# Two products' operands stay in SBUF, the other loads come three to a product from one list, and the splits of SwiGLU's results and the second norm's sums come later

## The chip, the cores and the metric

One core of a Trainium2 chip runs the kernel. The metric is the device time of one execution in microseconds (us); less is better.

## The reference

One layer of a hybrid decoder on x of 512 tokens by 2048 channels in float32. The input projection and the mixers come first and are not touched by the change. The change lies in the last line, the feed-forward part, with D_FF = 5632:

```python
h = rms_norm(x, norm1_g)
aq, ak, av, bu, bg, cq, ck, cv = split(h @ w_in)
mix = concat(dilated attention A, conformer convolution B, sliding attention C)
x = x + mix @ w_out
h2 = rms_norm(x, norm2_g)                       # "norm2": one factor per token
x = x + (silu(h2 @ w_gate) * (h2 @ w_up)) @ w_down
```

## The kernel before, in words

**Number form.** Each float32 operand of TensorE is split into a high part (fp32r) and the rest: for weights wh and wl (tiles of 128x1024), for activations two halves of one tile h or a. ScalarE (ACT) casts a weight tile twice, once into PSUM (wn, L275) and once into SBUF (wh, L276); VectorE (DVE) subtracts to get wl (L277). `split_up_to` does this two units ahead of use.

**Products.** The feed-forward matrix products are cut by a scheme of seven products for a 2x2 block product: instead of eight block products there are seven, on sums of blocks. They come in the order 5, 1, 7, 6, 2, 4, 3 (`ORDER`); below, "product 0" to "product 6" is the place in this order and "q" the number. The sums of weights, w('s'), w('21') and so on, are made by GpSimd (POOL, L211) from raw blocks w('11'), w('12'), w('21'), w('22') that SyncE (SP) loads at L259. The last number in such a name is the unit, of which a product has two. The sums of activations were made earlier and written to DRAM (hd, seven per pair of chunks).

**Steps.** 22 steps w0 to w21 (class `Wide`) make gate and up, eight steps d0 to d7 (class `Turned`) the first 16 pairs of chunks of the down product, and eight more (class `Down`) the rest. Each step w or d is seven products of 24 matmuls of 128x512 at L1383. Two steps, an odd w and the even one after it, use the same half of h: four of the eight pairs of chunks, so 4 x 7 = 28 tiles of 256 KB are in SBUF. In each even step w2 to w20, when a product has used its four tiles for the last time, these are freed, and one product later the four of the other half are loaded for the same q (`load_ops`, `h<-hd`, L1584). In w21 the same happens with four loads of a per product for d0 (`load_act`, `a<-od`, L1578).

**The results of two steps.** In an odd step g the blocks of gate and up get complete; `finish` (L1519 to L1521) makes silu(gate) x up for one of four blocks, turns it and sends it to DRAM (zd). At the end of the odd step each of the two chunks of features (named f with its number: f14 and f15 for w15) is set up to be read back, as `r` at one product's delay and as `l` at four (L1299, 64-element pieces), summed by POOL (`sums1`: ta, `sums2`: tb, L1307 to L1314), split by ACT and DVE (`piece`, L1319 to L1327) and stored to DRAM (od), from which the steps d load a. `piece3` splits r, `piece4` the needed half of l, `piece1` ta, `piece2` tb. The numbers in `PIECES_AT` are the delays in products of sums1, sums2, piece3, piece4, piece1, piece2, for the two chunks.

**What sets the order.** Everything is written out by hand in one program order, and each engine works through its own instructions in that order. `later(n, fn)` puts work into a queue that is run n products on, after the product's matmuls. SP issues all the transfers one after another. At each product `next_unit` also lets SP load the next raw blocks of weights as their buffers come free (`pump`). `slot` takes one of N_SLOTS tiles of 128x512; a tile is free again when its last reader is done.

**Norm2.** In w0, after product 2, `norm2` lets DVE copy the sums of squares (ssum2b, L1230) and TensorE add them over partitions (n2s, L355).

Of the kernel before, what the change touches and what calls it, by code (L numbers as in the profile page):

```python
# [16 lines left out]
T = 512  # L17
# [30 lines left out]
        "bg2 cq2 cq7 ak2 cq4 cq6 bu3 bg3 ak0 aq0 ak1 aq1 aq2 ak3 aq3").split()  # L48
ROWS = "c0 c3 c1 c5 c2 c7 c4 c6 a0 a1 b2 b1 b0 b3 a2 a3".split()

N_SLOTS = 67
N_WIDE = 4
COLUMN_BANKS = 2

# [23 lines left out]
J_SET = NJ // 2  # L78


PIECES_AT = ((5, 6, 2, 6, 6, 7), (6, 7, 4, 7, 8, 11))


BY = 4
# [42 lines left out]
def kernel(ctx: ExitStack, tc: tile.TileContext, xT, wi, wo, wgu, wd, cst_in, outT):  # L127
# [21 lines left out]
    def slot(name, dt=F32, cols=T):  # L149
        return sp.tile([P, cols], dt, name=name, tag="s")  # L150
# [78 lines left out]
    def set_of(g):  # L229
        return (g + 1) // 2 % 2  # L230
# [851 lines left out]
    def halves(t):  # L1082
        return t[:, :TH], t[:, TH:]
# [139 lines left out]

    outs = [(bank if i < 4 - COLUMN_BANKS else column)(f"out{i}") for i in range(4)]

    def norm2():
        b = psum["high"].tile([P, 1024], F32, name="n2s", tag="h")
        by_rows = slot("ssum2b")
        for v, to in zip(halves(ssum2), halves(by_rows)):
            nc.vector.tensor_copy(by_block(to), v.rearrange("p (a b c) -> p a b c", b=2, c=32))  # L1230
        n2["r"] = token_scale(by_rows, D, "n2", b[:, :NT])[1]

    acts = {}
    od = {p: tc.dram_tile([P, 7 * T], F32, name=f"od{p}") for p in range(NP)}
# [218 lines left out]
    class Wide(Turned):  # L1453
# [55 lines left out]
        def finish(self, at):  # L1509
            y, half = self.y.pop(at), int(at[1]) - 1  # L1510
            s, z = slot(f"s{self.g}_{at}"), slot(f"z{self.g}_{at}")
            gate = psum["high"].tile([P, 1024], F32, name=f"s{self.g}n{at}", tag="h")
            to = z.rearrange("p (b h c) -> p b h c", b=8, h=2)
            for h, t in enumerate(y):
                both = t.rearrange("p (f m d) -> p f m d", f=2, m=2)
                cols = slice(h * TH, (h + 1) * TH)
                act, out = (v[:, cols].rearrange("p (f d) -> p f d", f=2) for v in (gate, s))
                scale = n2["r"][:, 2 * half + h:2 * half + h + 1]
                nc.scalar.activation(act, both[:, :, 0], AF.Silu, scale=scale)  # L1519
                nc.vector.scalar_tensor_tensor(out, both[:, :, 1], scale, act, op0=ALU.mult, op1=ALU.mult)  # L1520
                nc.vector.transpose(to[:, :, h], s[:, cols].rearrange("p (c b) -> p b c", b=8))  # L1521
            later(0, nc.sync.dma_start, self.zd[at[0] == at[1]][{"12": 0, "21": 1, "22": 0, "11": 1}[at]], z,
                  queue=extras)
# [53 lines left out]
            at = LAID.index(q)  # L1577
            nc.sync.dma_start(acts[q, j].bitcast(F32), od[j][:, at * T:(at + 1) * T])  # L1578

    def load_ops(q, which):  # L1580
        for j in range(J_SET * which, J_SET * (which + 1)):
            ops[q, j] = slot(f"h{q}_{j}", F32R)
            at = LAID.index(q)
            nc.sync.dma_start(ops[q, j].bitcast(F32), hd[j][:, at * T:(at + 1) * T])  # L1584

    blk = None
    rest = [(q, j) for q in ORDER for j in range(TURNED, NP)]
    for g in range(G_STEPS + N_DOWN):
        t = g - G_STEPS
        turned = 0 <= t < N_TURNED  # L1590
        if t < 0:
            blk = Wide(g, blk)
        else:
            blk = (Turned if turned else Down)(t)
        for i, q in enumerate(ORDER):
            sums_now()
            run(evacs)
            for sub in range(BY // 2 if t < N_TURNED else 1):
                w = next_unit()
                if t < 0:  # L1600
                    first = J_SET * set_of(g) + 2 * sub
                    blk.multiply(i, sub, w, [ops[q, j] for j in range(first, first + 2)])
                    if ticks.due:
                        ticks.tick()
                elif turned:
                    first = BY * (t // 2) + 2 * sub
                    blk.multiply(i, sub, w, [acts[q, j] for j in range(first, first + 2)])
                else:
                    blk.multiply(q, w, [acts[q, j] for j in range(TURNED, NP)])
            if g == 0 and i == 2:  # L1610
                norm2()

            if t < 0 and (g % 2 == 0 or t == -1):
                for j in range(J_SET * set_of(g), J_SET * (set_of(g) + 1)):
                    ops.pop((q, j))
                if g == 0 and i == 0:
                    held.pop("x1"), held.pop("x3")
                    opening_ops.clear()
                if t == -1:
                    later(1, load_act, q, range(BY), queue=extras)  # L1620
                elif g:
                    later(1, load_ops, q, 1 - set_of(g), queue=extras)
            elif turned and t % 2:
                first = BY * (t // 2)
                for j in range(first, first + BY):
                    acts.pop((q, j))
                first += BY
                if first < TURNED:
                    later(1, load_act, q, range(first, first + BY), queue=extras)
            if N_TURNED - 2 <= t < N_TURNED:  # L1630
                n = 4 - (t % 2 == 0)
                for q2, j in rest[:n]:
                    later(1 if t % 2 else 0, load_act, q2, [j], queue=extras)
                del rest[:n]
            if i == (5 if turned else 3):
                load_y(t + 1)
            run(extras)
# [85 lines left out]
```

## Time and profile before

| what | value |
|---|---|
| median of 3 runs | 1888.57 us (1888.47 to 1890.7) |
| the profiled execution | 1890.46 us |
| its span, first to last instruction | 1888.7 us |
| mean granted clock of TensorE | 0.997 |
| read from HBM / written | 329.87 MB / 80.22 MB |
| loads h<-hd | 280 of 256 KB |

The profile is of one execution. TensorE's row (PE) in the stretches below is its matmuls alone; "[2.35 <-DVE ssum2b L1230]" behind an instruction says that its engine was idle for 2.35 us before it, and that a result of DVE's line 1230 ended that. PEclk is the share of full clock that TensorE was granted. SPq rows are the issue of a transfer, not its course.

### The profile page before, as it was taken

What the parts mean: (1) busy time and instruction counts of PE and PEld (TensorE: products, weight loads), DVE (VectorE), ACT (ScalarE), POOL (GpSimd) and SP (SyncE); (2) the same over time, 40 slices, a digit from 0 to 9 for tenths busy, and PEclk for the clock granted to TensorE, in tenths of its full rate; (3) what the DMA queues carried; (4) which work ended last, traced back from release to release, by engine and by line L of the source; (5) the groups of instructions that cost most, each with busy time, mean ns of one, the idle gap of its engine ahead of it and who ended that gap; (6) DMA issues with size and microseconds to landing.
All of it is one profiled execution on the core that took longest, in us unless ns stands there. A gap on an engine that the chain in (4) does not pass through costs nothing.

```text
span 1888.7 us, 26860 instructions
## 1 busy us (share of the span) xinstructions
PE 1861.3 (99%) x8548; PEld 1539.6 (82%) x8548; DVE 1530.9 (81%) x2318; ACT 1360.4 (72%) x1956; POOL 1083.9 (57%) x681
## 2 busy tenths in 40 slices
PE   9999999999999999999999999999999899999999
PEld 7888888888887887788887888878887788888888
DVE  7688899897578788788887888978878677778887
ACT  6234555555456788888888888888877887777775
POOL 6013445362253458576585765856757676776786
PEclk9999999999999999999999999999999999999999
DMA  6334333433396377989879898798979595678984
GB/s 258 134 106 117 96 95 101 117 123 117 115 321 238 108 231 258 291 263 312 261 253 300 262 309 266 245 310 263 310 243 349 179 335 184 206 244 284 310 242 124
DMA packets 330077, 419.49 MB, mean 222 GB/s; under 512 B 82256, under 2 KB 211408, under 8 KB 329936
## 3 DMA queue, kind: packets, MB, share of 16 engines
q1 hardware_dynamic: 329792, 417.77, 68.6%
q8 instruction: 68, 1.11, 0.2%
q14 instruction: 73, 0.60, 0.1%
q10 hardware_dynamic: 144, 0.01, 0.0%
HBM read 329.87 MB, written 80.22 MB: 217 GB/s over the span
## 4 chain that ended last, share of the span: by engine, by line
PE 78%; DMA 5%; DVE 5%; ACT 4%; POOL 3%; issue 2%; SPq 2%; DVEq 0%; POOLq 0%; ACTq 0%
PE out L1383 44%; PE out L1275 6%; PE o L313 2%; PE o L315 2%; PE o L314 2%; DMA h<-hd 2%; PE cq L313 2%; PE cq L314 2%; PE cq L315 2%; SPq L1584 1%; DVE G L1483 1%; ACT wn L275 1%; DMA a<-od 1%; DVE wl L277 1%; ACT wh L276 1%
## 5 line engine op out<-in xcount | busy, mean ns | idle before, releaser
L1383 PE MATMUL out<-wh,h 128*128 128x512 f32 x2464 | 616.1, 392 | 11.2 <-ACT wh L276 10.1
L1383 PEld LDWEIGHTS out<-wh,h 128*128 128x128 f32 x2464 | 462.0, 188 | 118.2 <-ACT wh L276 19.2
L1383 PE MATMUL out<-wl,h 128*128 128x512 f32 x1232 | 330.2, 390 | 0.0
L1383 PEld LDWEIGHTS out<-wl,h 128*128 128x128 f32 x1232 | 231.8, 188 | 48.4
L1383 PE MATMUL out<-wh,a 128*128 128x512 f32 x896 | 223.3, 391 | 7.3 <-ACT wh L276 7.2
L1383 PEld LDWEIGHTS out<-wh,a 128*128 128x128 f32 x896 | 168.2, 188 | 45.3 <-ACT wh L276 10.2
L1383 PE MATMUL out<-wl,a 128*128 128x512 f32 x448 | 120.6, 391 | 0.0
L1383 PEld LDWEIGHTS out<-wl,a 128*128 128x128 f32 x448 | 84.7, 189 | 17.7
L515 DVE SCALAR_TENSOR_TENSOR y<-bu,cst,y 128x511 f32<-128x511 f32 (+14 forms) x120 | 93.8, 781 | 1.4
L1486 DVE TENSOR_TENSOR G<-G,out 128x512 f32<-128x512 f32 x132 | 83.6, 674 | 3.9 <-PE out L1383 3.9
L271 ACT CAST wh<-w 128x1024 fp32r<-128x1024 f32 (+1 forms) x41 | 42.1, 1031 | 57.8 <-PE o L314 36.1
L1275 PE MATMUL out<-a,wh 128*128 128x512 f32 x330 | 80.1, 391 | 0.0
L291 ACT CAST wh<-w 128x1024 fp32r<-128x1024 f32 x52 | 54.7, 1052 | 32.1 <-PE bg L314 9.0
L295 DVE TENSOR_TENSOR wl<-w,wh 128x1024 fp32r<-128x1024 f32 x52 | 65.3, 1257 | 14.1 <-ACT wh L291 13.9
L1483 DVE TENSOR_TENSOR G<-G,out 128x512 f32<-128x512 f32 x110 | 68.4, 679 | 1.7 <-PE out L1383 1.7
L1275 PEld LDWEIGHTS out<-a,wh 128*128 128x128 f32 x330 | 60.2, 188 | 11.4
L1521 DVE STREAM_TRANSPOSE z<-s 128x256 f32<-128x256 f32 x88 | 59.8, 680 | 3.0
L272 DVE TENSOR_TENSOR wl<-w,wh 128x1024 fp32r<-128x1024 f32 (+1 forms) x41 | 51.6, 1261 | 9.4 <-ACT wh L271 9.0
L313 PE MATMUL o<-mh_c,wh 128*128 128x512 f32 x128 | 51.3, 401 | 0.0
L314 PE MATMUL o<-ml_c,wh 128*128 128x512 f32 x128 | 50.2, 392 | 0.1
L315 PE MATMUL o<-mh_c,wl 128*128 128x512 f32 x128 | 50.1, 391 | 0.0
L1275 PEld LDWEIGHTS out<-a,wl 128*128 128x128 f32 x330 | 43.3, 191 | 2.2
(2758 smaller groups left out, 5112.0 us busy)
## 6 DMA issues: line engine op xcount, KB each, us to landing
h<-hd SPq DMA_DIRECT2D x280, 256.0 KB, 5.3
od<-a SPq DMA_DIRECT2D x154, 256.0 KB, 6.2
a<-od SPq DMA_DIRECT2D x154, 256.0 KB, 6.0
w<-in_wi SPq DMA_DIRECT2D x59, 512.0 KB, 3.3
w<-in_wo SPq DMA_DIRECT2D x32, 512.0 KB, 3.4
hd<-h SPq DMA_DIRECT2D x56, 256.0 KB, 5.2
zd<-z SPq DMA_DIRECT2D x44, 256.0 KB, 4.9
x<-in_xT SPq DMA_DIRECT2D x16, 256.0 KB, 7.2
```

The lines of the kernel that those rows point to most:

```text
L272: eng.tensor_sub(lo[:, :n], t[:, :n], hi[:, :n].bitcast(F32))
L291: nc.scalar.copy(hi, t)
L295: nc.vector.tensor_sub(lo, t, hi.bitcast(F32))
L313: nc.tensor.matmul(out, wh, xh, start=start, stop=False)
L314: nc.tensor.matmul(out, wh, xl, start=False, stop=False)
L315: nc.tensor.matmul(out, wl, xh, start=False, stop=stop)
L515: nc.vector.scalar_tensor_tensor(yconv[j][:, i:], hconv[j][:, :T - i], c, yconv[j][:, i:], op0=ALU.mult, op1=ALU.add)
L1275: nc.tensor.matmul(out, lhs[:, s], rhs, start=begin, stop=last and low == flip[0] and x is xs[-1], skip_group_check=True)
L1383: nc.tensor.matmul(to[h], x[:, h * P:(h + 1) * P], v[:, j], start=sub == 0 and h not in started, stop=sub == 1 and n in (len(todo) - 1, le ...
L1483: op(t, t, b)
L1486: nc.vector.tensor_add(t, t, b)
L1521: nc.vector.transpose(to[:, :, h], s[:, cols].rearrange("p (c b) -> p b c", b=8))
```

## The change

- `KEEP`: the tiles of h of products q = 1 and q = 7 stay in SBUF for both halves of the chunks, so that from w2 on they are not loaded again; h<-hd goes from 280 to 208 transfers. (At w20 the kept ones are freed and loaded once more.)
- `LOADS`: the other loads of h go into one list, from which each product takes three; in w21 the 28 loads of a for d0 are put at the end of the same list, which still holds seven loads of h then.
- `PIECES_AT`: piece3 of the two chunks moves from delays 2 and 4 to 4 and 5; piece4 from 6 and 7 to 5 and 6; sums2 comes right behind sums1.
- `finish`: both silus are written ahead of DVE's two products.
- `norm2` is cut in two: DVE's copies stay behind product 2 of w0, TensorE's sum comes behind product 5.
- One more slot.

```diff
@@ -48,7 +48,7 @@
         "bg2 cq2 cq7 ak2 cq4 cq6 bu3 bg3 ak0 aq0 ak1 aq1 aq2 ak3 aq3").split()
 ROWS = "c0 c3 c1 c5 c2 c7 c4 c6 a0 a1 b2 b1 b0 b3 a2 a3".split()
 
-N_SLOTS = 67
+N_SLOTS = 68
 N_WIDE = 4
 COLUMN_BANKS = 2
 
@@ -78,7 +78,9 @@
 J_SET = NJ // 2
 
 
-PIECES_AT = ((5, 6, 2, 6, 6, 7), (6, 7, 4, 7, 8, 11))
+KEEP = (1, 7)
+LOADS = 3
+PIECES_AT = ((5, 5, 4, 5, 6, 7), (6, 6, 5, 6, 8, 11))
 
 
 BY = 4
@@ -1223,12 +1225,14 @@
 
     outs = [(bank if i < 4 - COLUMN_BANKS else column)(f"out{i}") for i in range(4)]
 
-    def norm2():
+    def norm2a():
+        n2["s"] = slot("ssum2b")
+        for v, to in zip(halves(ssum2), halves(n2["s"])):
+            nc.vector.tensor_copy(by_block(to), v.rearrange("p (a b c) -> p a b c", b=2, c=32))
+
+    def norm2b():
         b = psum["high"].tile([P, 1024], F32, name="n2s", tag="h")
-        by_rows = slot("ssum2b")
-        for v, to in zip(halves(ssum2), halves(by_rows)):
-            nc.vector.tensor_copy(by_block(to), v.rearrange("p (a b c) -> p a b c", b=2, c=32))
-        n2["r"] = token_scale(by_rows, D, "n2", b[:, :NT])[1]
+        n2["r"] = token_scale(n2.pop("s"), D, "n2", b[:, :NT])[1]
 
     acts = {}
     od = {p: tc.dram_tile([P, 7 * T], F32, name=f"od{p}") for p in range(NP)}
@@ -1511,13 +1515,16 @@
             s, z = slot(f"s{self.g}_{at}"), slot(f"z{self.g}_{at}")
             gate = psum["high"].tile([P, 1024], F32, name=f"s{self.g}n{at}", tag="h")
             to = z.rearrange("p (b h c) -> p b h c", b=8, h=2)
+            args = []
             for h, t in enumerate(y):
                 both = t.rearrange("p (f m d) -> p f m d", f=2, m=2)
                 cols = slice(h * TH, (h + 1) * TH)
                 act, out = (v[:, cols].rearrange("p (f d) -> p f d", f=2) for v in (gate, s))
                 scale = n2["r"][:, 2 * half + h:2 * half + h + 1]
                 nc.scalar.activation(act, both[:, :, 0], AF.Silu, scale=scale)
-                nc.vector.scalar_tensor_tensor(out, both[:, :, 1], scale, act, op0=ALU.mult, op1=ALU.mult)
+                args.append((h, cols, act, out, scale, both[:, :, 1]))
+            for h, cols, act, out, scale, up in args:
+                nc.vector.scalar_tensor_tensor(out, up, scale, act, op0=ALU.mult, op1=ALU.mult)
                 nc.vector.transpose(to[:, :, h], s[:, cols].rearrange("p (c b) -> p b c", b=8))
             later(0, nc.sync.dma_start, self.zd[at[0] == at[1]][{"12": 0, "21": 1, "22": 0, "11": 1}[at]], z,
                   queue=extras)
@@ -1577,11 +1584,12 @@
             at = LAID.index(q)
             nc.sync.dma_start(acts[q, j].bitcast(F32), od[j][:, at * T:(at + 1) * T])
 
-    def load_ops(q, which):
-        for j in range(J_SET * which, J_SET * (which + 1)):
-            ops[q, j] = slot(f"h{q}_{j}", F32R)
-            at = LAID.index(q)
-            nc.sync.dma_start(ops[q, j].bitcast(F32), hd[j][:, at * T:(at + 1) * T])
+    def load_op(q, j):
+        ops[q, j] = slot(f"h{q}_{j}", F32R)
+        at = LAID.index(q)
+        nc.sync.dma_start(ops[q, j].bitcast(F32), hd[j][:, at * T:(at + 1) * T])
+
+    loads = []
 
     blk = None
     rest = [(q, j) for q in ORDER for j in range(TURNED, NP)]
@@ -1607,19 +1615,20 @@
                     blk.multiply(i, sub, w, [acts[q, j] for j in range(first, first + 2)])
                 else:
                     blk.multiply(q, w, [acts[q, j] for j in range(TURNED, NP)])
-            if g == 0 and i == 2:
-                norm2()
+            if g == 0 and i in (2, 5):
+                (norm2a if i == 2 else norm2b)()
 
             if t < 0 and (g % 2 == 0 or t == -1):
                 for j in range(J_SET * set_of(g), J_SET * (set_of(g) + 1)):
-                    ops.pop((q, j))
+                    if q not in KEEP or t >= -2:
+                        ops.pop((q, j))
+                        if 0 < g and t < -1:
+                            loads.append((load_op, q, J_SET * (1 - set_of(g)) + j % J_SET))
+                    if t == -1:
+                        loads.append((load_act, q, [j % J_SET]))
                 if g == 0 and i == 0:
                     held.pop("x1"), held.pop("x3")
                     opening_ops.clear()
-                if t == -1:
-                    later(1, load_act, q, range(BY), queue=extras)
-                elif g:
-                    later(1, load_ops, q, 1 - set_of(g), queue=extras)
             elif turned and t % 2:
                 first = BY * (t // 2)
                 for j in range(first, first + BY):
@@ -1627,6 +1636,9 @@
                 first += BY
                 if first < TURNED:
                     later(1, load_act, q, range(first, first + BY), queue=extras)
+            for fn, *args in loads[:LOADS]:
+                later(1, fn, *args, queue=extras)
+            del loads[:LOADS]
             if N_TURNED - 2 <= t < N_TURNED:
                 n = 4 - (t % 2 == 0)
                 for q2, j in rest[:n]:
```

What this does to the engines' own order, at the places that matter (a line number grows by 2 to 8 between the two files: L259 is L261 after the change, L1241 L1245, L1299 L1303, L1383 L1387, L1584 L1590).

SyncE, from w16's product 3 on, when f14r has been read; h tiles are those of the next two steps, od the stores of split pieces. Before:

```order
L1241 DMA zd_0_11732<-z_12_12205 128x512
L1584 DMA h_4_12329<-hd_3893 128x512
L1584 DMA h_5_12331<-hd_3894 128x512
L1584 DMA h_6_12333<-hd_3895 128x512
L1584 DMA h_7_12335<-hd_3896 128x512
L1241 DMA od_5843<-a_14_12269 128x512
L1241 DMA od_5843<-a_14_12272 128x512
L259 DMA w('22', 'w17', 1)_12349<-in_wgu 128x4x256
L259 DMA w('11', 'w17', 0)_12351<-in_wgu 128x4x256
L259 DMA w('11', 'w17', 1)_12353<-in_wgu 128x4x256
L259 DMA w('12', 'w17', 0)_12355<-in_wgu 128x4x256
L1299 DMA f14l<-zd_0_11732 128x8x64
```

After:

```order
L1590 DMA h_7_12153<-hd_3896 128x512
L1245 DMA zd_0_11622<-z_12_12093 128x512
L261 DMA w('22', 'w17', 1)_12211<-in_wgu 128x4x256
L261 DMA w('11', 'w17', 0)_12213<-in_wgu 128x4x256
L261 DMA w('11', 'w17', 1)_12215<-in_wgu 128x4x256
L261 DMA w('12', 'w17', 0)_12217<-in_wgu 128x4x256
L1303 DMA f14l<-zd_0_11622 128x8x64
L1303 DMA f15l<-zd_0_11622 128x8x64
L1590 DMA h_4_12263<-hd_3893 128x512
```

The raw block w('22') of w17's second unit, on which POOL's sum waits, now stands behind four instead of twelve loads of h and ahead of the od stores; the loads of f14l and f15l come with it.

GpSimd, at the end of w16; ta and tb are the sums of f14 and f15. Before:

```order
L211 TENSOR_TENSOR w('s', 'w17', 1)_12429<-w('21', 'w17', 1)_12190,w('22', 'w17', 1)_12349 128x1024
L1307 TENSOR_TENSOR f14ta<-f14r,f14l 128x256
L1308 TENSOR_TENSOR f14ta<-f14l,f14r 128x256
L211 TENSOR_TENSOR w('21', 'w17', 0)_12168<-w('21', 'w17', 0)_12168,w('11', 'w17', 0)_12351 128x1024
L211 TENSOR_TENSOR w('21', 'w17', 1)_12190<-w('21', 'w17', 1)_12190,w('11', 'w17', 1)_12353 128x1024
L1313 TENSOR_TENSOR f14tb<-f14ta,f14r 128x256
L1314 TENSOR_TENSOR f14tb<-f14tb,f14l 128x256
```

After:

```order
L213 TENSOR_TENSOR w('s', 'w17', 1)_12289<-w('21', 'w17', 1)_12078,w('22', 'w17', 1)_12211 128x1024
L1311 TENSOR_TENSOR f14ta<-f14r,f14l 128x256
L1312 TENSOR_TENSOR f14ta<-f14l,f14r 128x256
L1317 TENSOR_TENSOR f14tb<-f14ta,f14r 128x256
L1318 TENSOR_TENSOR f14tb<-f14tb,f14l 128x256
L213 TENSOR_TENSOR w('21', 'w17', 0)_12056<-w('21', 'w17', 0)_12056,w('11', 'w17', 0)_12213 128x1024
L213 TENSOR_TENSOR w('21', 'w17', 1)_12078<-w('21', 'w17', 1)_12078,w('11', 'w17', 1)_12215 128x1024
```

f14tb comes ahead of two sums of weights instead of behind them.

ScalarE, just ahead of w17's first casts. Before:

```order
L275 CAST wn_12468<-w('s', 'w17', 0)_12369 128x1024
L276 CAST wh_12466<-w('s', 'w17', 0)_12369 128x1024
L275 CAST wn_12487<-w('s', 'w17', 1)_12429 128x1024
L276 CAST wh_12485<-w('s', 'w17', 1)_12429 128x1024
L1319 CAST f14n_12505<-f14l 128x256
L1326 CAST a_14_12507<-f14l 128x4x2x32
```

After:

```order
L278 CAST wh_12291<-w('s', 'w16', 1)_11911 128x1024
L1323 CAST f14n_12315<-f14l 128x256
L1330 CAST a_14_12317<-f14l 128x4x2x32
L1323 CAST f15n_12320<-f15r 128x512
L1330 CAST a_15_12322<-f15r 128x4x2x32
L1330 CAST a_15_12325<-f15r 128x4x2x32
L277 CAST wn_12341<-w('s', 'w17', 0)_12231 128x1024
L278 CAST wh_12339<-w('s', 'w17', 0)_12231 128x1024
L277 CAST wn_12360<-w('s', 'w17', 1)_12289 128x1024
L278 CAST wh_12358<-w('s', 'w17', 1)_12289 128x1024
```

The pieces of f14l and f15r now stand ahead of the casts of w17's first unit, where f14l's came behind both units' casts before, and f15r's earlier still.

SyncE in d0, from its product 4 on; a tiles are d0's operands, f20 and f21 the last two chunks. Before:

```order
L1241 DMA od_5849<-a_20_14715 128x512
L1241 DMA od_5849<-a_20_14718 128x512
L259 DMA w('22', 'd1', 1)_14781<-in_wd 128x4x256
L259 DMA w('11', 'd1', 0)_14783<-in_wd 128x4x256
L259 DMA w('11', 'd1', 1)_14785<-in_wd 128x4x256
L259 DMA w('12', 'd1', 0)_14787<-in_wd 128x4x256
L1299 DMA f20l<-zd_0_14126 128x8x64
L1299 DMA f21l<-zd_0_14126 128x8x64
L1241 DMA od_5850<-a_21_14827 128x512
L1241 DMA od_5850<-a_21_14830 128x512
```

After:

```order
L1585 DMA a_2_14601<-od_5831 128x512
L261 DMA w('22', 'd1', 1)_14617<-in_wd 128x4x256
L261 DMA w('11', 'd1', 0)_14619<-in_wd 128x4x256
L261 DMA w('11', 'd1', 1)_14621<-in_wd 128x4x256
L261 DMA w('12', 'd1', 0)_14623<-in_wd 128x4x256
L1303 DMA f20l<-zd_0_13978 128x8x64
L1303 DMA f21l<-zd_0_13978 128x8x64
L1585 DMA a_3_14669<-od_5832 128x512
L1585 DMA a_0_14671<-od_5829 128x512
L1585 DMA a_1_14673<-od_5830 128x512
L1585 DMA a_2_14734<-od_5831 128x512
L1585 DMA a_3_14736<-od_5832 128x512
```

Before the change all 28 loads of a were issued by the end of d0's product 1, ahead of these rows. After it the last ones, a_3 of product 5 and four of product 6, stand behind four raw blocks of weights and two chunks.

## The prediction

> **What bounds the kernel now.** I read the page first (busy shares, DMA issues), then the stretches of TensorE's matmul line L1383 by step, then the waits and the timeline at each place where a step is longer than it need be.
>
> ```profile
> PE 1861.3 (99%) x8548; PEld 1539.6 (82%) x8548; DVE 1530.9 (81%) x2318; ACT 1360.4 (72%) x1956; POOL 1083.9 (57%) x681
> h<-hd SPq DMA_DIRECT2D x280, 256.0 KB, 5.3
> ```
>
> TensorE is busy 99% of the span, and the change takes no matmul away. So it can only win the time in which TensorE waits or runs at a lowered clock, and only in the steps it touches. The stretches below are TensorE's matmuls of L1383 in w0, w1, w2 to w20, w21, d0 and d1 (stretch, its length, busy, granted clock, DMA share, GB/s):
>
> ```profile
> 587.49:632.35 44.86, 41.08 (x169) 0.92 0.54 173
> 632.35:670.43 38.08, 38.08 (x170) 1.00 0.38 118
> 670.43:1410.28 739.85, 731.53 (x3194) 1.00 0.87 275
> 1410.28:1452.05 41.77, 38.92 (x170) 1.00 0.93 322
> 1452.05:1500.65 48.60, 41.47 (x169) 0.96 0.83 265
> 1500.65:1539.54 38.89, 38.67 (x170) 1.00 0.70 244
> ```
>
> w1 is a clean step: 38.08 us, 5.44 for each of its seven products. Against that w0 loses 44.86 - 38.08 = 6.8, the 19 steps w2 to w20 lose 739.85 - 19 x 38.08 = 16.3, w21 3.7, d0 10.5 and d1 0.8. Together 38.1 us: no change in these steps can save more.
>
> **Norm2.** In w0 TensorE's small product n2s stands right behind VectorE's copies of the sums:
>
> ```profile
> 604.68 1.79 DVE L1230 COPY ssum2b<-ssum 128x256 f32<-128x256 f32 x2
> 606.33 1.56 PE L355 MATMUL n2s<-ones,ssum2b 128*128 128x1 f32 x8 [2.35 <-DVE ssum2b L1230]
> 607.75:613.45 5.70, 5.70 (x15) 4.44 (x16) 2.62 (x5) 2.86 (x3) 5.28 (x3) 0.50 0.08 29
> ```
>
> TensorE waits 2.35 us, and the next 5.70 us (all engines; PE first) run at a granted clock of 0.50, so about half of them, 2.4 to 2.9, is lost too. After the change n2s comes three products, 16 us, after the copies, and finds them done. What stays is n2s itself, about 1.4 with its pipeline. Its wait and half clock make 4.75 to 5.2, and w0's whole loss is 6.8; I take 5.5, with 4.4 (wait and 2.0 of clock) and 6.8 as ends. The split adds one DVE operand held for three products and no instruction.
> The Trainium skill ("TensorE: Matmul & The Clock Gate", Part 1) says that the clock falls after about 3.4 us of idling. By that rule a wait of 2.35 would cost no clock and the gain would be about 3; the row above, 0.50 after a wait of 2.35, disagrees, and the row decides.
>
> **Steps w2 to w20: two waits per pair of steps.** An example from w16 (even) and w17 (odd):
>
> ```profile
> 1227.00:1272.00 45.00, 43.74 (x191) 35.25 (x190) 34.30 (x50) 37.76 (x53) 24.71 (x16) 1.00 0.97 302
> 1233.68 0.59 ACT L1319 CAST f14n<-f14r 128x512 fp32r<-128x512 f32 x1 [2.12 <-DMA f14r<-zd]
> 1234.21 0.71 ACT L1326 CAST a<-f14r 128x256 fp32r<-128x256 f32 x2
> 1237.84 2.09 PE L1383 MATMUL out<-wh,h 128*128 128x512 f32 x8
> 1237.76 2.57 SPq L1584 DMA_DIRECT2D h<-hd  x4
> 1242.63 0.38 SPq L259 DMA_DIRECT2D w('22', 'w17', 1)_12349<-in_wgu  x1
> 1245.21 2.68 SPq L1299 DMA_DIRECT2D f14l<-zd  x1
> 1249.24 1.06 ACT L276 CAST wh<-w('s', 'w17', 0)_12369 128x1024 fp32r<-128x1024 f32 x1
> 1249.60 2.40 POOL L211 TENSOR_TENSOR w('s', 'w17', 1)_12429<-w('21', 'w17', 1)_12190,w('22', 'w17', 1)_12349 128x1024 f32<-128x1024 f32 x1 [11.02 <-DMA w('22', 'w17', 1)_12349<-in_wgu]
> 1255.12 0.38 ACT L1319 CAST f14n<-f14l 128x256 fp32r<-128x256 f32 x1 [1.08 <-DMA f14l<-zd]
> 1261.29 0.76 POOL L1313 TENSOR_TENSOR f14tb<-f14ta,f14r 128x256 f32<-128x256 f32 x1
> 1262.90 0.59 ACT L1319 CAST f14n<-f14tb 128x512 fp32r<-128x512 f32 x1 [1.23 <-POOL f14tb L1314]
> 1266.76 2.41 PE L1383 MATMUL out<-wh,h 128*128 128x512 f32 x8 [1.18 <-ACT wh L276]
> ```
>
> First wait: ScalarE reaches the piece of f14r 2.12 us before that has landed, and the casts of weights queue behind it. The change puts this piece two products (10.9 us) later, behind the casts, so the wait goes (ten steps). Second: SP issues w22 of w17 behind twelve loads of h, 4.8 us after product 4's start (1242.63 - 1237.84); POOL waits 11.02 for it and f14l comes after it; ScalarE then waits for f14l, and for f14tb, whose POOL sums stand behind two weight sums of 2.4. TensorE's wait at 1266.76 is the end of that chain. The change puts w22 ahead of eight h loads and of two od stores, and f14tb ahead of the weight sums, so these causes go as well.
>
> What is late next? ScalarE now takes the piece of f14l before, not after, the casts of w17's first operand, with f15r's piece between them. TensorE needs those casts 3 x 5.44 = 16.3 after product 4's start. They take 2.0 (two at about 1 us, row 1249.24), f15r's piece 1.24 (1234.21 + 0.71 - 1233.68), f14l's, half as wide, 0.7: so f14l must have landed 12.4 after product 4's start. Now it landed at 1255.12, that is 17.3 after (4.8 to w22's issue, then 12.5). The second part, without the loads ahead, is bounded by d1's row below, where f20l was used 11.2 after w22's issue (1498.27 - 1487.08). The first lies between 0 and 4.8; w22 still needs its buffer, which ScalarE gives up earlier by the wait removed (2.1): 4.8 - 2.1 = 2.7, less some of the queue: 2.0 I take. 2.0 + 11.2 = 13.2, and since POOL's use at 1498.27 was also waiting for TensorE, f20l had landed before that; I take 12.9. New wait: 0.5 per pair (0 with an issue at once, 3.6 with 4.8 + 11.2). With 0.3 of small leftovers a pair loses 0.8 where it lost 16.3 / 9.5 = 1.7: 9.5 x 0.9 = 8.6 saved. Ends: 16.3 saved (nothing left), or a loss (rival 3).
>
> Of the other edits here: KEEP takes 72 of the 280 loads away; at a DMA share of 0.97 around the waits that is what moves w22 up, and it is not counted twice. The silus written together remove a wait of ScalarE (under 1 us, not ended by TensorE) and make VectorE's first product wait for both silus, half a microsecond; both lie beside matmuls: nothing, plus or minus 0.5 in all. The extra buffer issues nothing.
>
> **w21** is the same second wait at its worst (3.7), with POOL behind a later w22; I take 2.7 saved, from 0 to 3.7.
>
> **d0.**
>
> ```profile
> 1424.00:1480.00 56.00, 50.98 (x216) 40.15 (x216) 42.02 (x58) 43.13 (x59) 35.37 (x20) 1.00 1.00 338
> 1445.33 0.38 SPq L259 DMA_DIRECT2D w('22', 'd0', 1)_14371<-in_wd  x1
> 1453.98 1.02 ACT L275 CAST wn<-w('s', 'd0', 1)_14449 128x1024 fp32r<-128x1024 f32 x1 [5.72 <-POOL w('s', 'd0', 1)_14449 L211]
> 1478.43 0.59 ACT L1319 CAST f20n<-f20r 128x512 fp32r<-128x512 f32 x1 [3.46 <-DMA f20r<-zd]
> 1482.58 2.68 PE L1383 MATMUL out<-wh,a 128*128 128x512 f32 x8 [3.71 <-ACT wh L276]
> 1482.58:1487.50 4.92, 4.92 (x15) 3.92 (x16) 4.01 (x6) 4.92 (x6) 2.06 (x2) 0.65 0.00 0
> 1487.08 0.38 SPq L259 DMA_DIRECT2D w('22', 'd1', 1)_14781<-in_wd  x1
> 1489.74 3.20 SPq L1299 DMA_DIRECT2D f21l<-zd  x1
> 1498.27 0.74 POOL L1307 TENSOR_TENSOR f20ta<-f20r,f20l 128x256 f32<-128x256 f32 x1 [3.04 <-PE out L1383]
> ```
>
> Around the 28 loads of a the DMA share is 1.00. Two waits cost 10.5: w22 of d0 behind twelve loads (ScalarE waits 5.72), and f20r's piece (3.46, TensorE 3.71, then a clock of 0.65, 0.35 x 4.92 = 1.7). With three loads per product from one list w22 is issued behind two loads of a, and f20r's piece comes two products later: about 9.7 of the 10.5 go, the rest being like d1's 0.8.
> But the list still holds seven loads of h when the loads of a begin, so they end later: a of product 5's last tile (a4_3) is now issued behind w22, both w11, w12, f20l and f21l of d1. TensorE needs it halfway through product 5, 5.44 + 3.7 = 9.1 after product 4's start. Its predecessors: w22 issued 2.5 after product 4's start (between 0 and now's 1487.08 - 1482.58 = 4.5); f20l in use 11.2 later, f21l and a4_3 behind it about 1.4: 15.1. TensorE would wait 6.0, then lose about 2 of clock (by the two rows of 0.50 and 0.65 above: 1.7 to 2.9), and before that about 1.3 at product 3's a6_2, behind f20r and f21r: 9.3 to 10, so d0 gains 0. Ends: 9.7 gained when these loads land in time, 2.5 lost when w22 is issued at 4.5 (a wait of 8.0), the clock takes 2.9 and a6_2 its 1.3.
> By the same part of that page of the Trainium skill ("TensorE: Matmul & The Clock Gate", Part 1), full clock is back after about 3.4 us of sustained work, which would make the clock's share of that wait 1.7; an estimate that changes the sum by 0.3.
>
> **Sum.** -5.5 (norm2) - 8.6 (w2 to w20) - 2.7 (w21) + 0 (d0) = -16.8. The profiled execution took 1890.46 (span 1888.7 and 1.8 around it), 1.9 above the median of the runs, 1888.57; the sum is of its own steps, and I take it from the median: 1871.8.
>
> **Rivals.**
> 1. The new wait for f?l eats the steady gain (1.4 instead of 0.5 per pair, landing 13.8 after product 4's start): w2 to w20 save nothing, the rest 8.2: 1880. For it: 4.5 in d0, where the queue was empty, is the only unloaded issue I have. Against: there it was late because TensorE and the casts were.
> 2. The loads of a arrive in time, since the seven h loads ahead are quick: d0 gives 9.7 more: 1862. For it: d0 then has fewer od stores ahead; against: the order of SP's queue, where a4_3 stands seventh from w22.
> 3. Slower: at before's pace (4.8 + 12.5) f?l lands 17.3 after product 4's start, 4.9 too late on each of 9.5 pairs: 46 + 3 against 16.3, +33, less 8.2: 1913; half of that lateness gives about 1890. The sign turns where 9.5 x (wait + 0.3) = 16.3 + 8.2, a wait of 2.3, that is a landing 14.7 after product 4's start. Against: eight h loads of 0.25 MB no longer stand ahead.
> 4. No change within 0.2% (3.8 us, about what a measurement of this kernel can tell): the wait is 1.9 to 2.7 a pair, or d0's is twice as long as reckoned with rival 1: 1885 to 1892.
>
> **Chances.** Forecast (1866 to 1877) 0.52; rival 1, 0.17; rival 2, 0.16; rival 4, 0.08; rival 3, 0.07. The first three are faster by over 0.2%: 0.85; same 0.08; slower 0.07. Range: from rival 2 to just past rival 1, 1861 to 1882, leaves out rivals 3 and 4 and little of the others.
>
> **What the profile after would show.** Norm2: w0 near 39.4, no wait at n2s, a clock of 1.00. w2 to w20: 731 us in all; no wait of ScalarE for f?r, POOL's wait for w22 under 8, ScalarE's for f?l up to 1. w21: 39. d0: no wait for f20r, but one of TensorE for a in product 5 with a lowered clock behind it. Wrong, if SP issues w22 more than 4 us after product 4's start, if f?l waits exceed 2, or if d0 is a clean 39.

## The result and the profile after

The changed kernel took a median of 1878.52 us (1877.12 to 1879.82, four runs) against 1889.63 (1888.47 to 1890.87, four runs): a ratio of 0.9941, 95% interval 0.9924 to 0.9958, or 11.1 us less. The forecast was 16.8 less, a time of 1871.8 in a range of 1861 to 1882. The profiled execution took 1877.44 (span 1875.2), 13.0 less than the profiled one of before; the steps below account for its span.

The same stretches as before the change, TensorE's matmuls (now line L1387) in w0, w1, w2 to w20, w21, d0 and d1:

```profile
585.30:624.97 39.67, 38.92 (x168) 1.00 0.60 195
624.97:663.05 38.08, 38.08 (x169) 1.00 0.38 118
663.05:1397.84 734.79, 727.36 (x3193) 1.00 0.80 252
1397.84:1436.18 38.34, 38.34 (x169) 1.00 0.95 326
1436.18:1487.89 51.71, 42.86 (x170) 0.90 0.85 275
1487.89:1525.97 38.08, 38.08 (x170) 1.00 0.87 297
```

The granted clock in w0 went from 0.92 to 1.00, in d0 from 0.96 down to 0.90. By place, with the forecast beside it:

| place | before | after | change | forecast |
|---|---|---|---|---|
| start of w0 | 587.49 | 585.30 | -2.2 | 0 |
| w0 (norm2) | 44.86 | 39.67 | -5.2 | -5.5 |
| w2 to w20 | 739.85 | 734.79 | -5.1 | -8.6 |
| w21 | 41.77 | 38.34 | -3.4 | -2.7 |
| d0 | 48.60 | 51.71 | +3.1 | 0 |
| d1 | 38.89 | 38.08 | -0.8 | 0 |
| sum | | | -13.6 | -16.8 |

The waits of TensorE in the whole execution show what is left, and where:

```profile
PE out L1387 <- DMA a<-od: 8.8, 2, 4.9
PE out L1387 <- ACT wh L278: 7.3, 9, 1.5
```

No wait for n2s any more; two waits for loads of a, both in d0, which before the change did not exist; and nine for ScalarE's casts, at the ends of even steps. The chain behind these is seen in w16 and w17, the pair shown before, where TensorE's wait is the shortest of the nine (timeline rows of SyncE, GpSimd, ScalarE and TensorE; the number in brackets is idle time and what ended it; the last two rows are the longest and the shortest of ScalarE's ten waits for f?l, the `l` piece of a pair's first chunk):

```profile
1228.18 0.38 SPq L261 DMA_DIRECT2D w('22', 'w17', 1)_12211<-in_wgu  x1
1230.62 0.82 SPq L1303 DMA_DIRECT2D f14l<-zd  x1
1233.67 2.41 POOL L213 TENSOR_TENSOR w('s', 'w17', 1)_12289<-w('21', 'w17', 1)_12078,w('22', 'w17', 1)_12211 128x1024 f32<-128x1024 f32 x1 [6.66 <-DVE wl L279]
1238.89 0.38 ACT L1323 CAST f14n<-f14l 128x256 fp32r<-128x256 f32 x1 [4.45 <-DMA f14l<-zd]
1242.69 2.11 PE L1387 MATMUL out<-wh,h 128*128 128x512 f32 x8 [0.28 <-ACT wh L278]
ACT f10n L1323 <- DMA f10l<-zd: 5.7, 1, 5.7
ACT f12n L1323 <- DMA f12l<-zd: 4.3, 1, 4.3
```

Product 4 of w16 starts at 1225.94. w22 is issued 2.2 after that (before: 4.8), POOL no longer waits for it, f14r's piece waits for nothing; but ScalarE, which now takes f14l's piece ahead of w17's first casts, waits 4.45 for f14l to land, which it uses 12.95 after product 4's start, and TensorE waits for the casts behind it. In d0:

```profile
1459.35 3.53 PE L1387 MATMUL out<-wh,a 128*128 128x512 f32 x8 [3.97 <-DMA a<-od]
1477.85 2.07 PE L1387 MATMUL out<-wh,a 128*128 128x512 f32 x4 [4.87 <-DMA a<-od]
1452.35 4.86 SPq L1585 DMA_DIRECT2D a<-od  x3
1465.97 0.38 SPq L261 DMA_DIRECT2D w('22', 'd1', 1)_14617<-in_wd  x1
1472.26 4.36 SPq L1585 DMA_DIRECT2D a<-od  x5
1459.35:1463.75 4.40, 4.40 (x13) 3.50 (x13) 0.26 (x1) 1.13 (x2) 0.00 (x0) 0.61 0.99 357
1477.85:1484.24 6.39, 6.39 (x16) 5.01 (x17) 2.85 (x5) 3.08 (x4) 6.31 (x5) 0.56 0.85 304
```

The wait of 3.97 is in product 3, for a6_2, which by the order of the 28 loads is the first of the three issued from 1452.35. The wait of 4.87 is in product 5: the last five loads of a, issued from 1472.26, stand behind w22 of d1 (1465.97) and what follows it. The last two rows are the stretches behind the two waits, all engines, with the granted clock third from the end: 0.61 and 0.56.

### The profile page after: what moved, and what is told of

The parts are those of the page before. It is cut to its first block, busy times and chain, and to the rows that moved or that the text cites. A ratio compares the mean times of both kernels' runs of the same rounds, so it can differ in the third digit from the quotient of the medians.

```text
span 1875.2 us, 26746 instructions
## 1 busy us (share of the span) xinstructions
PE 1853.6 (99%) x8548; PEld 1539.9 (82%) x8548; DVE 1533.1 (82%) x2318; ACT 1366.0 (73%) x1956; POOL 1082.9 (58%) x681
## 4 chain that ended last, share of the span: by engine, by line
PE 93%; DMA 4%; ACT 1%; issue 1%; DVE 0%; SPq 0%; ACTq 0%; DVEq 0%
PE out L1387 56%; PE out L1279 6%; PE o L316 3%; PE o L315 3%; PE o L317 3%; PE cq L315 2%; PE cq L316 2%; PE cq L317 2%; PE in L316 1%; PE ak L315 1%; PE aq L315 1%; PE ak L317 1%; PE aq L317 1%; PE ak L316 1%; PE bu L316 1%; PE bu L315 1%
## 5 line engine op out<-in xcount | busy, mean ns | idle before, releaser
L1387 PE MATMUL out<-wh,h 128*128 128x512 f32 x2464 | 611.4, 390 | 7.5 <-ACT wh L278 7.3
L1387 PEld LDWEIGHTS out<-wh,h 128*128 128x128 f32 x2464 | 460.8, 188 | 109.5 <-ACT wh L278 13.9
L1387 PE MATMUL out<-wl,h 128*128 128x512 f32 x1232 | 329.3, 389 | 0.0
L1387 PEld LDWEIGHTS out<-wl,h 128*128 128x128 f32 x1232 | 231.3, 188 | 48.2
L1387 PE MATMUL out<-wh,a 128*128 128x512 f32 x896 | 225.0, 394 | 8.8 <-DMA a<-od 8.8
L1387 PEld LDWEIGHTS out<-wh,a 128*128 128x128 f32 x896 | 170.3, 190 | 45.2 <-DMA a<-od 5.3
L1387 PE MATMUL out<-wl,a 128*128 128x512 f32 x448 | 120.7, 392 | 0.0
L1387 PEld LDWEIGHTS out<-wl,a 128*128 128x128 f32 x448 | 85.0, 190 | 17.8
L1432 DVE TENSOR_TENSOR Y<-Y,out 128x512 f32<-128x512 f32 x48 | 30.8, 682 | 20.6 <-PE out L1387 20.4
```

Of the source, the lines that this page charges most:

```text
L1387: nc.tensor.matmul(to[h], x[:, h * P:(h + 1) * P], v[:, j], start=sub == 0 and h not in started, stop=sub == 1 and n in (len(todo) - 1, le ...
```

## The experiments

All changed lines are those of the diff above, on the kernel before or after it. One profile each, unless a ratio is given. Runs of the kernel before took 1887.7 to 1893.7 us beside these, so single times differ by up to some 6 us with nothing changed, and the argument goes by the stretches.

### 1. Norm2's split alone, on the kernel before

```diff
-            if g == 0 and i == 2:
-                norm2()
+            if g == 0 and i in (2, 5):
+                (norm2a if i == 2 else norm2b)()
```

> The kernel before with only the split of norm2. If the loss of w0 is the wait for the copies and the half clock behind it, w0 takes 39.7 us as in the changed kernel (before 44.9), and all else stays: w2 to w20 739.9, w21 41.8, d0 48.6; in all 5.2 us less. Rival: w0's other loss (the first step's own waits) only moves, and w0 stays above 42.

Measured: 1884.83 beside 1892.97 of the kernel before, one run each; w0 39.65, and w2 to w20 as before, 740.59 (stretches of TensorE's matmuls of w0 and of w2 to w20):

```profile
588.32:627.97 39.65, 38.91 (x168) 1.00 0.61 196
666.05:1406.64 740.59, 731.45 (x3194) 1.00 0.87 275
```

So w0's 5.2 us come with norm2's split alone. Their size is not fixed, though: in four more profiles with norm2 unsplit w0 took 43.20, 43.24, 44.66 and 43.22 (experiments 2, 3 and, twice, 9), behind the same wait of 2.3 to 2.4 us, at a granted clock of 0.92 to 0.96 over w0. The 44.86 of the kernel before is the longest of the five, and the split is worth 3.5 to 5.2. w21 and d0, which this edit does not touch, took 39.20 and 50.01, together 1.2 less than before: these steps vary by that much and more between profiles (see experiment 9).

### 2. The new PIECES_AT alone, on the kernel before

```diff
-PIECES_AT = ((5, 6, 2, 6, 6, 7), (6, 7, 4, 7, 8, 11))
+PIECES_AT = ((5, 5, 4, 5, 6, 7), (6, 6, 5, 6, 8, 11))
```

> The kernel before with only the new PIECES_AT: all 280 loads of h, four per product. Theory: the landing of f?l is set by the h loads ahead of w22; with the piece of f?l ahead of the casts of the odd step's first operand and the old pace (landing 17.3 after product 4's start, deadline 12.4) TensorE loses 4.9 per pair: w2 to w20 about 770 us, in all about 30 us slower than before. Rival: f?l lands by its own latency once ScalarE no longer waits for f?r, and the loads of h matter little: w2 to w20 about 735 as in the changed kernel.

Measured: 1904.11 beside 1892.97 of the kernel before in the same session. w2 to w20 took 762.73, 22.9 more than before, and d0 41.40, 7.2 less:

```profile
669.06:1431.79 762.73, 734.19 (x3193) 0.99 0.84 268
1471.61:1513.01 41.40, 38.83 (x170) 1.00 0.90 289
ACT f0n L1319 <- DMA f0l<-zd: 8.1, 1, 8.1
```

ScalarE waits 6.2 to 8.1 for f?l in each pair (the last row is the longest of ten, from its waits). In w2 to w20 the theory holds (762.73 for about 770) and its rival falls: with all the loads ahead of w22, the earlier piece of f?l costs. TensorE loses 762.73 - 723.52 = 39.2 there, 4.1 per pair, where 4.9 and small leftovers were expected. In all the kernel is only 11.1 slower, not about 30: the theory did not reckon with what d0 and other steps gain. In d0 TensorE's wait of 3.71 behind f20r is gone, with the lowered clock behind it, which goes with the later piece of f20r; ScalarE's wait for the sum with w22 is also shorter, 3.1 for 5.72.

### 3. KEEP, LOADS and the slot, without the rest

```diff
+KEEP = (1, 7)
+LOADS = 3
-N_SLOTS = 67
+N_SLOTS = 68
```

and the code of the list; norm2, the pieces and the silus as before.

> The kernel before with only KEEP, LOADS and the extra slot; norm2, the pieces and the silus as before. Theory: w22 comes early, so the second wait of a pair shrinks, while ScalarE's wait for f?r (2.1 to 2.9) stays: w2 to w20 728 to 733, better than the 734.8 of the changed kernel, since the piece of f?l stays behind the casts. d0 has the late loads of a: 49 to 52. w0 44.9. Rival: the two waits for f?l and f?r are worth the same, and w2 to w20 take 735 or more.

Measured: 1890.99 beside 1892.97. w2 to w20 took 743.77, not 728 to 733:

```profile
666.69:1410.46 743.77, 731.09 (x3193) 1.00 0.78 248
1448.94:1501.94 53.00, 43.53 (x170) 0.90 0.85 275
822.38:865.08 42.70, 40.03 (x169) 0.96 0.68 198
865.08:903.16 38.08, 38.08 (x169) 1.00 0.86 290
ACT f4n L1321 <- DMA f4r<-zd: 3.3, 1, 3.3
```

The third and fourth rows are w6 and w7, one of the two worst pairs. The odd step is clean, as the theory said; but the even one has grown to 42.70, with ScalarE waiting 3.3 for f4r. Over all of w2 to w20 the odd steps lose 1.6 us, where they lost 10.7 before, and the even ones 18.6, where they lost 5.6; w6 and w12 make half of that, and the other even steps lose 0.6 to 1.8 each. The theory's figure falls and the rival holds: alone, earlier weights gain nothing against before and 0.6 to 2.6 against the slot alone (experiment 9), because what the odd steps no longer lose the even ones lose at the piece of f?r. Neither edit alone is worth the 5 us of both together. d0 has the changed kernel's late loads of a already.

### 4. The changed kernel with finish as before

```diff
-            args = []
-                args.append((h, cols, act, out, scale, both[:, :, 1]))
-            for h, cols, act, out, scale, up in args:
-                nc.vector.scalar_tensor_tensor(out, up, scale, act, op0=ALU.mult, op1=ALU.mult)
+                nc.vector.scalar_tensor_tensor(out, both[:, :, 1], scale, act, op0=ALU.mult, op1=ALU.mult)
```

> The changed kernel with finish as before (silu, product, turn, for one half after the other). Theory: hidden beside matmuls, w2 to w20 within 1 us of 734.8, w21 within 0.5 of 38.3. Rival: the odd steps' 0.1 us at products 1 and 2 and part of the waits come or go with it, over 2 us in all.

Measured: 1876.52; the stretches w2 to w20 and w21:

```profile
662.86:1397.93 735.07, 727.31 (x3194) 1.00 0.80 252
1397.93:1436.27 38.34, 38.34 (x169) 1.00 0.93 325
```

Within 0.3 of the changed kernel: the order of the silus is worth nothing here.

### 5. The changed kernel without eight needless loads

```diff
-                        if 0 < g and t < -1:
+                        if 0 < g and t < -1 and q not in KEEP:
```

At w20 the tiles of q = 1 and 7 for w21 are in SBUF already, and the changed kernel loads them a second time.

> The changed kernel without the eight loads of h in w20 and w21 that fetch tiles of q = 1 and 7 which are in SBUF already; the list is then shorter by eight when the loads of a are put on it. Theory: both waits of TensorE for a in d0 (3.97 and 4.87, with lowered clock behind each) come from those eight: the loads of a for q = 6, 2 and 4 then stand ahead of f20l, and d0 takes 38 to 41 us instead of 51.7; in all 11 to 13 us less than the changed kernel. Rival: the loads of a are late by the transfers' own pace beside weights and stores, and d0 stays above 46.

Measured: 1869.23, that is 8.2 less than the changed kernel's profiled execution, where 11 to 13 were expected. d0 took 45.48, between theory and rival:

```profile
1434.70:1480.18 45.48, 40.46 (x170) 0.96 0.92 296
1459.33 1.19 PE L1387 MATMUL out<-wh,a 128*128 128x512 f32 x4 [1.56 <-DMA a<-od]
1473.90 0.38 ACT L1323 CAST f20n<-f20l 128x256 fp32r<-128x256 f32 x1 [6.84 <-DMA f20l<-zd]
1475.78 3.66 PE L1387 MATMUL out<-wh,a 128*128 128x512 f32 x8 [3.46 <-ACT a L1330]
```

The waits for a shrink from 8.8 to 1.6, so the eight loads made most of them, as the theory said. It missed what is late next: 26 of the 28 loads of a now stand ahead of f20l, where 23 did, ScalarE waits 6.84 for f20l, and TensorE 3.46 behind it.

### 6. The changed kernel with f?l read one product earlier

```diff
-                    later(4, one.load, "l", self.zd[0], queue=extras)
+                    later(3, one.load, "l", self.zd[0], queue=extras)
```

> The changed kernel with f?l loaded one product earlier, which puts it ahead of w22, both w11 and w12 on SP's queue. Theory: f?l landed 10.7 us after w22's issue because four transfers of 0.5 MB stand ahead; now it lands about 4 to 6 us earlier, ScalarE's wait of 4.3 to 5.7 and TensorE's wait at the end of even steps go: w2 to w20 about 726 (734.8 in the changed kernel). Rival: SP waits for the store of z that f?l reads, w22 is issued late behind it, POOL's sum of w('s') is late instead, and w2 to w20 take 734 or more.

Measured: 1869.20. w2 to w20 are clean to the last matmul, 723.52 or 19 x 38.08, and d0 is longer:

```profile
662.80:1386.32 723.52, 723.52 (x3194) 1.00 0.80 254
1424.40:1480.21 55.81, 45.54 (x170) 0.88 0.82 272
1226.08 0.37 ACT L1323 CAST f14n<-f14l 128x256 fp32r<-128x256 f32 x1
1227.83 2.41 POOL L213 TENSOR_TENSOR w('s', 'w17', 1)_12289<-w('21', 'w17', 1)_12078,w('22', 'w17', 1)_12215 128x1024 f32<-128x1024 f32 x1 [9.10 <-DVE a L1331]
PE out L1387 <- DMA a<-od: 9.4, 3, 5.1
```

f14l is there when ScalarE comes to it at 1226.08, 8.4 after product 4's start (1217.68), where it was awaited until 12.95; POOL's sum waits for VectorE, not for w22. What was left in w2 to w20 was f?l's place on SP's queue, behind four transfers of 0.5 MB. But d0 gives 4.1 of the 11.3 back (55.81 against 51.71): TensorE comes to d0 11.8 us earlier, but the three loads with a6_2 are issued only 8.6 us earlier (at 1443.79 for 1452.35).

### 7. The changed kernel with f?l's piece behind the casts, as before

```diff
-PIECES_AT = ((5, 5, 4, 5, 6, 7), (6, 6, 5, 6, 8, 11))
+PIECES_AT = ((5, 5, 4, 6, 6, 7), (6, 6, 5, 7, 8, 11))
```

> The changed kernel with piece4 (f?l) one product later, behind the casts of the odd step's first operand, as before the change. Theory: what is left in w2 to w20 is the wait for f?l ahead of those casts, so w2 to w20 fall from 734.8 to 725 to 729. Rival: the wait only moves one product on and is lost at product 1 or 2 of the odd step: 733 or more.

Measured: 1871.05.

```profile
663.59:1387.64 724.05, 724.02 (x3193) 1.00 0.81 254
1425.72:1482.02 56.30, 43.39 (x170) 0.91 0.87 278
```

w2 to w20 take 724.05, a little under the theory's 725 to 729, and the wait does not move on. So the earlier piece4 is the step of the change that costs, 10.7 us, and the other edits together would have given 15.8 there. d0 gives 4.6 back, as in experiment 6.

### 8. The changed kernel with four loads of a per product

```diff
-                    if t == -1:
-                        loads.append((load_act, q, [j % J_SET]))
+                if t == -1:
+                    later(1, load_act, q, range(BY), queue=extras)
```

> The changed kernel with the loads of a for d0 as before the change: four per product as each product of w21 ends, beside what is left of the list of h. Theory: TensorE's waits for a in d0 go, and the old wait of w22 of d0 behind loads of a comes back in part (the seven h loads ahead, fewer od stores): d0 41 to 47 us. Rival: it is as long as before the change (48.6) or longer, since h and a loads now go out seven per product at w21's start.

Measured: 1875.76.

```profile
1399.88:1441.15 41.27, 38.88 (x168) 1.00 0.93 329
1441.15:1484.42 43.27, 39.65 (x169) 1.00 0.93 300
1484.42:1524.64 40.22, 38.96 (x168) 1.00 0.72 246
PE out L1387 <- DMA h<-hd: 2.4, 2, 2.0
```

d0 43.27, in the theory's span, with no wait for a. But w21 and d1 are 2.9 and 2.1 longer: of d0's 8.4 us some 3.4 are left over the three steps. In w21 TensorE now waits for loads of h, twice (the last row: 2.4 in all, the longer 2.0), in the step in which, as the rival has it, loads of h and a go out seven per product; in d1 it waits for ScalarE's casts again. (w2 to w20, ahead of this edit, took 737.19, 2.4 more than in the changed kernel's first profile.)

### 9. The 68th slot alone, on the kernel before

```diff
-N_SLOTS = 67
+N_SLOTS = 68
```

> The kernel before with only the 68th slot. In every profile with 68 slots w0 starts at 585.0 to 585.8 us, in every one with 67 at 587.5 to 588.3, though no other part of the change acts before w0. Theory: the slot alone does this, by a wait that an engine has for a slot to come free in the mixers (VectorE's 2.36 for the transfer aq<-aq2hi): w0 starts at 585.0 to 585.8, and w0 to d7 are as before (44.9, 739.9, 41.8, 48.6). Rival: it is a difference between executions: 587.5 or more.

> The kernel before with only the 68th slot, once more and timed. In one profile it brought w0 2.1 us earlier and made w2 to w20 746.3 instead of 739.9. Theory: both are the slot's, since loads and tiles now fall on other slots: w0 starts at 585 to 586, w2 to w20 take 744 to 748, and the time is that of the kernel before or up to 0.2% longer. Rival: the longer steps were that one execution's, w2 to w20 take 739 to 741, and the kernel is 2 us (0.1%) faster than before.

Measured, first profile: w0 starts at 585.39, w2 to w20 take 746.34; this single run took 1893.24, beside 1888.51 of the kernel before (nine runs). Timed: 1888.55 (1884.5 to 1891.02, 11 runs) beside 1891.14 of before, a ratio of 0.9986 (0.9976 to 0.9997). In that kernel's second profile w0 starts at 585.31 and w2 to w20 take 744.42. The rows are a VectorE instruction of the mixers before, with the slot alone and in the changed kernel, and the stretches of w0 and of w2 to w20 with the slot alone, second profile:

```profile
367.56 0.69 DVE L860 TENSOR_TENSOR a0pl<-a0t,a0ph 128x512 fp32r<-128x512 f32 x1 [2.36 <-DMA aq<-aq2hi]
365.45 0.69 DVE L860 TENSOR_TENSOR a0pl<-a0t,a0ph 128x512 fp32r<-128x512 f32 x1
365.50 0.69 DVE L862 TENSOR_TENSOR a0pl<-a0t,a0ph 128x512 fp32r<-128x512 f32 x1
585.31:628.53 43.22, 39.95 (x169) 0.96 0.56 179
666.61:1411.03 744.42, 731.82 (x3193) 1.00 0.87 274
```

The first run's theory held for w0's start and failed for the steps, which it had as before. Both parts of the second run's theory hold in both profiles: the slot ends a wait in the mixers and brings w0 2.1 earlier, and w2 to w20 are some 4 to 6.5 us longer with 68 slots (744.42 and 746.34) than with 67 (739.85, and 740.59 in experiment 1). The time is 0.14% below before, not equal or longer as the theory had it; in the time the rival was right. In that second profile w0 is 1.6 shorter than before, and w21 and d0 together 3.7 shorter (39.36 and 47.34), as they already varied in experiment 1. Why the slot makes the steps longer was not followed to an instruction; loads and tiles fall on other slots and so wait for other readers, which is argued, not shown.

### 10. What the runs point to

The changed kernel with experiments 5 and 6, and for the last pair (f20, f21, read only after d7) everything four products later:

```diff
+LAST = 4
+                    d = LAST if self.g == G_STEPS - 1 else 0
-                    later(1, one.load, "r", self.zd[1], queue=extras)
-                    later(4, one.load, "l", self.zd[0], queue=extras)
+                    later(1 + d, one.load, "r", self.zd[1], queue=extras)
+                    later(3 + d, one.load, "l", self.zd[0], queue=extras)
```

(the pieces' delays get + d too.)

> The changed kernel with f?l one product earlier, without the eight needless loads, and for the last pair (f20, f21, whose results are read only after d7) reading back and pieces four products later. Theory: w2 to w20 are clean (723.5) as with f?l earlier; in d0 the loads of a are early, and f20l no longer stands in front of the casts of d1: d0 38 to 41 us; in all 1852 to 1856 us, 22 to 26 less than the changed kernel. Rival: d0 loses by w22 of d0 behind loads of a, as before the change (ScalarE waited 2.76 for it without the eight loads), or d1 takes over the waits: d0 and d1 together above 82, in all 1859 or more.

> The changed kernel once more, on the same chip and against the same runs of the kernel before: a ratio of 0.992 to 0.996 as measured first, with w0 starting at 585 and w2 to w20 734.8. Rival to the whole reading: the 11 us were the chip's state, and the ratio is above 0.997.

Measured: 1851.91 (1851.52 to 1852.78, four runs), ratio to before 0.9804 (0.9791 to 0.9817); the changed kernel in the same session 1877.69, ratio 0.9939 (0.9926 to 0.9953). The kernel of this experiment beats both, by 36.6 and 25.8 us. w2 to w20, w21, d0 and d1, and its busy shares:

```profile
662.74:1386.25 723.51, 723.51 (x3193) 1.00 0.79 254
1386.25:1424.33 38.08, 38.08 (x169) 1.00 0.90 316
1424.33:1462.41 38.08, 38.08 (x169) 1.00 0.92 304
1462.41:1500.57 38.16, 38.16 (x170) 1.00 0.82 270
PE 1844.4 (100%) x8548; PEld 1538.7 (83%) x8548; DVE 1535.5 (83%) x2318; ACT 1371.1 (74%) x1956; POOL 1082.8 (59%) x681
```

From w1 to d7 TensorE waits for nothing: the ceiling of 38.1 us named in the prediction is taken but for norm2's own 1.6 and d1's 0.1. The longer stall that the rival expected in d0 or d1 did not come. The three edits were run together only, so what the later reading of f20 and f21 gives by itself no run shows. The changed kernel's second profile has w2 to w20 at 735.92 and d0 at 52.02.

## Why the prediction was right, and where not

**Right: the direction and the places.** Norm2 gave 5.2 of the 5.5 reckoned, alone as together (experiment 1), and the granted clock of w0's matmuls is 1.00 where it was 0.50 behind the wait of 2.35. Against the five profiles with norm2 unsplit the gain is 4.2 on average, so the 5.5 lies above the whole span of 3.5 to 5.2. w21 gave 3.4 for 2.7, but it also took only 39.2 and 39.36 where no edit was meant for it (experiments 1 and 9), so how much of this is the change's is not shown. The new wait for f?l, named as what is late next, is there, and its place was reckoned closely: w22 2.2 after product 4's start for 2.0, f14l in use 12.95 after it for 12.9. The silus cost nothing (experiment 4).

One of the prediction's own signs of being wrong came: ScalarE's waits for f?l, expected up to 1 and wrong above 2, are 4.3 to 5.7. In w16 ScalarE comes to the piece 8.5 us after product 4's start, 3.9 before the deadline of 12.4, and only what lies behind the deadline costs TensorE time. So the deadline held in this pair, and this sign left out the time that ScalarE has to spare.

**Too small: the new wait per pair.** Its deadline and landing were taken from one pair, and in that pair, w16 and w17, TensorE lost 0.7 where 0.8 was reckoned. The other pairs lose more: over the ten even steps TensorE loses about 0.9 each (0.3 to 1.6), over the odd steps 0.25. Together 11.3 stayed where 7.7 were reckoned, the 3.5 by which the term was too large. Experiments 6 and 7 show that nearly all of it is the wait for f?l: with that out of the way 0.0 and 0.5 are left. So the term mis-sized is the new wait, 1.1 to 1.2 per pair for 0.5, while the 0.3 of leftovers is not there. Why f?l is later in some pairs than in others stays open.

Rival 1 was half true: w2 to w20 saved 5.1, not 8.6 and not 0. The measured 1878.5 lies in the stated range, but nearer to this rival's 1880 than to the forecast, and outside the 1866 to 1877 to which the forecast's chance of 0.52 was given. Experiments 2 and 3 say why the account was so tight: neither edit gains alone. The loads alone (experiment 3) move the wait from f?l to f?r (w6 grew to 42.70), the pieces alone (experiment 2) from f?r to f?l (8.1 at worst).

**Too small: the loads of a.** The term was 9.3 to 10 lost against 9.7 gained; 13.6 were lost (51.71 - 38.08). The rows account for it: waits of 4.87 and 3.97, and behind them an estimated 2.8 (0.44 x 6.39) and 1.7 (0.39 x 4.40) of lowered clock, 13.4 in all. The a4_3 wait was put at 6.0 and about 2 of clock and took 4.87 and 2.8, since it landed 14.1 after product 4's start (1477.85 - 1463.75), for 15.1. The a6_2 wait, put at 1.3, took 3.97 and 1.7 of clock. That is the term mis-sized: 1.3 was reckoned for f20r and f21r ahead of it, where the loads of a as a whole were behind, by the eight needless ones (experiment 5). Rival 2 did not come. That eight of the loads in front were needless the prediction did not see, though the list's seven left loads were its own reckoning.

**Missed: the slot.** "Issues nothing" was true and the conclusion was not. The slot ended a 2.36 us wait of VectorE far from the change's place, and with it alone w2 to w20 are longer (experiment 9). Against the slot alone (744.4 and 746.3) the changed kernel's 734.8 in w2 to w20 is a gain of 10 to 12, more than the 8.6 forecast; against 739.85 it is 5.1. That the slot took back the 3.5 that are missing is not shown, and experiments 6 and 7 speak against it: with the same 68 slots next to nothing is lost in w2 to w20 once f?l is out of the way. No run has the changed kernel with 67 slots.

**The sum** is 5.7 too large (16.8 for 11.1). By places it is 3.2 too large: w2 to w20 are 3.5 too good, d0 3.1 and norm2 0.3, and against that stand the earlier start of w0 (2.2), w21 (0.7) and d1 (0.8). The 2.2 were forecast by nobody; that they covered part of the two misses is luck. The profile's own fall was 13.0; the two profiled executions lie 0.8 above and 1.1 below their medians, which is the rest.

## What to carry to other kernels

When loads are moved on a shared queue, read its order up to each transfer that an engine will wait for next, and set the time at which that transfer lands against the time by which it is needed, in more than one place: here one pair gave 0.7 us lost and the average was 1.2. Two edits that each gain nothing can gain together, and a part of one can still cost (here 10.7 us were lost by one piece placed one product too early). A list that carries several kinds of loads must be followed to its end: the change's own backlog of eight needless loads delayed the next stage, and a stage that gets faster reaches it earlier, so some of the gain was given back there. A longer pool of buffers is not free of effect: one slot more moved the time of stages far from the edit, most likely because each new tile then waits for another earlier reader, which no run here follows.

## What the runs showed of the hardware

In the kernel before, a wait of 2.35 us of TensorE was followed by a granted clock of 0.50 over the next 5.7 us, and in the changed kernel waits of 3.97 and 4.87 by 0.61 and 0.56 over the next 4.4 and 6.4; waits of 1.2 us and less, in w17 before, left 1.00. The loss behind one and the same wait is not fixed: with norm2 unsplit, w0 took 43.2 to 44.9 us in five profiles, at a granted clock of 0.96 to 0.92. From the issue of w22 until f14l was used, 10.7 us passed (1228.18 to 1238.89): four transfers of 0.5 MB and f14l, 0.25 MB in 64-element pieces, were issued in a row, on an SP queue that had issued nothing for 5.8 us, with f15l and loads of h behind them.
